# Layer 2's recurrence on two heads a tile: direction pairs become head pairs, and the inverse is folded into the step

## The chip, the cores and the metric

The kernel runs on one core of one Trainium2 chip. The metric is the device time of one execution in microseconds. The engines are TensorE (PE in the rows, PEld for its weight loads), VectorE (DVE), ScalarE (ACT), GpSimd (POOL) and SyncE (SP), which issues the transfers.

## The reference

Three transformer layers run on one sequence of 512 tokens, with 256 context tokens in the first two; the width is 1024. The change touches layer 2 only, a recurrence with 16 heads of 64, run forward and backward over the context and then over the sequence:

```python
def step(S, inp):                       # S: 64 x 64 for each head
    w_t, k_t, v_t, kk_t, kka_t = inp[:5]
    S = (S * w_t[:, :, None, :]
         - jnp.einsum('bhij,bhj->bhi', S, kk_t)[..., None] * kka_t[:, :, None, :]
         + v_t[..., None] * k_t[:, :, None, :])
    y = jnp.einsum('bhij,bhj->bhi', S, inp[5]) if emit else None
    return S, y
...
for d, reverse in enumerate((False, True)):
    s_ctx, y_c = wkv_scan(s0, decay_c, k_dc, v_c, kk_c, a_c, r_c, reverse)
    _, y_d = wkv_scan(s_ctx, decay, k_d, v, kk, a, r, reverse)
y = rwkv_readout(ys[0] + ys[1], r, dirs[0][1] + dirs[1][1], v, g, r_k, ln_g, ln_b, wo, h.dtype)
```

The readout normalizes y by head, adds a bonus (sum of r, k and r_k over a head, times v), multiplies by the gate g and projects by wo.

## The kernel before

The 768 steps are cut into 12 chunks of 64 (4 of the context, 8 of the sequence). Within a chunk the recurrence is a triangular solve, so that a chunk needs a few 64 x 64 products, the inverse of a unit triangular matrix, and one state that is passed on. A block is two heads; there are eight blocks. The scheduler of the framework orders each engine's instructions ahead of the run, from program order and a model of its own; tiles in pools with a number of buffers set which work may run ahead.

The features are made first (`features`): decays, keys, rates and r are projected, written to memory by head with the backward direction reversed (`rev`), and the values v are written by token (`vt`). While the value projections still run, `Scan.front(0)` starts. Then `layer1` calls `rest` for block 0, and `front(blk)`, `rest()` for the blocks 1 to 7.

`front` (L304 on) works on one head at a time with the two directions on the halves of the 128 partitions: it loads the head's tensors, scans the log decays (L361), takes their exponentials (P at L364, inverse decays at L366), makes keys and rates (L368 to L377), fills the tiles G with products (L387, L390), and makes the chunk products on TensorE (L329), which masks move from PSUM into G (L332, L337) and copies into Ld (L334, L335). Transposes (L344, L346) complete G. There are three sets of G (`self.hp[blk % 3]`), and two of Ld. The bonus sum goes through memory (`bd`).

`rest` (L408 on) masks Ld on GpSimd (L421), transposes it on VectorE so that 96 small triangles lie on the partitions (L422), inverts their 32 x 32 diagonal parts by 60 instructions on GpSimd (L427, L428), transposes back (L432, L433) and assembles the 64 x 64 inverses T from 32 x 32 matmuls in PSUM bank f (L443 to L457). `fold` multiplies T into the transposed keys and the outputs' products in place (L467, L471). Then come 12 steps: a chunk's values and state lie together in a tile ZU, filled by transfers (L483); a step is a first group of matmuls (L501) into a bank b of this block's parity, two copies (ScalarE L503, VectorE L504), a second group with an identity that carries the state (L508, L509), and two multiplies by the chunk's decay (L512). The output Y gathers in a bank y, of which there are two (L520). The last part copies Y (L524), makes the norm's statistics in the same bank (L530 to L541) and writes the block out (L546). For block 7 the output projection of the blocks 0 to 5 is woven between its steps (`interleave`, L1288), with its weights in the room that `scan.fp` has left.

The lines that set how far blocks may run ahead:

```python
self.p.psum_swap(("mm", "v"), b0=1, b1=1, y=2)
G = self.hp[blk % 3].tile([128, 8 if g else 4, 4, CH], F32, name="G", tag=f"G{g > 0}", bufs=4 if g else 2)
Ld = self.lp[blk % 2 == 0].tile([128, 32, 64], F32, name="Ld", tag="Ld")
ps = self.p.pt(f"b{blk % 2}")
```

## Time and profile before

| | us |
|---|---|
| median of three runs (3163.01 to 3174.26) | 3166.6 |
| the profiled execution | 3169.68 |
| its span, first to last instruction | 3167.8 |
| TensorE busy | 2825.9 |
| VectorE busy | 1786.6 |
| ScalarE busy | 1552.0 |
| GpSimd busy | 1138.5 |

The mean granted TensorE clock is 0.923 of full speed. The feature projections of layer 2 run from about 1050 to 1268 us of the span, front and values together to about 1400, the blocks of the recurrence to 1980. Times in the rows count from the span's start. A row of a timeline merges neighbouring instructions of one line ("x8"), and its duration goes to the end of the last; an fp32 matmul is two instructions. "Idle before" is the time in which an engine waited, with what ended it.

### The profile page before, as it was taken

Reading aid. Unit: us, or ns where it says so; the run is one execution under the profiler, and the core shown is the slowest. Engines: PE = TensorE matmul, PEld = TensorE weight load, DVE = VectorE, ACT = ScalarE, POOL = GpSimd, SP = SyncE. Lnnn points to the kernel's source line nnn. Section 1 sums busy time; section 2 is a strip of 40 time slices with the busy share of each in tenths; the row PEclk is TensorE's granted clock in tenths of the full one; section 3 lists DMA queues with packets and bytes.
Section 4 is the critical chain, followed back from the end, with each engine's and each line's share of the span. In section 5 each row is a group of like instructions: output and inputs, shape, how many; then the busy total and the mean of one; then the engine's idle time right before and its main releaser. Section 6 shows DMA issues by size and latency. Waiting matters only on the chain.

```text
span 3167.8 us, 50960 instructions
## 1 busy us (share of the span) xinstructions
PE 2825.9 (89%) x19290; PEld 2343.8 (74%) x19290; DVE 1786.6 (56%) x3557; ACT 1552.0 (49%) x3104; POOL 1138.5 (36%) x1500
## 2 busy tenths in 40 slices
PE   6999889999996899886777769699997999989999
PEld 6967778888885688764666658577876885678887
DVE  8466383444448725758688732644456654556364
ACT  3246556666664633554566532455543444544341
POOL 4013436667675212045666640245543110010000
PEclk9989989999998899987688879799998996999999
DMA  5323213333331565432223231244541220022222
GB/s 224 127 82 98 104 50 128 117 126 127 113 114 61 190 194 156 162 123 84 73 96 103 79 113 53 99 171 170 179 150 56 80 87 7 14 80 90 103 96 85
DMA packets 137589, 345.69 MB, mean 109 GB/s; under 512 B 16385, under 2 KB 48769, under 8 KB 120065
## 3 DMA queue, kind: packets, MB, share of 16 engines
q1 hardware_dynamic: 137344, 342.43, 31.6%
q8 instruction: 153, 2.51, 0.3%
q14 instruction: 92, 0.75, 0.1%
HBM read 293.35 MB, written 49.02 MB: 108 GB/s over the span
## 4 chain that ended last, share of the span: by engine, by line
PE 34%; DVE 8%; ACT 6%; POOL 5%; DMA 4%; issue 2%; SPq 0%; ACTq 0%; POOLq 0%; DVEq 0%
PE mm L590 7%; PE mm L591 7%; PE mm L592 7%; POOL acc L733 2%; DMA adaw<-in_ada_dram 2%; PE a L1288 2%; ACT wh L583 1%; PE st L1247 1%; PE a L329 1%; POOL M L428 1%; POOL Mt L427 1%; PE y L520 1%; DVE G L387 1%; PE a L1920 1%; PE a L1923 1%
## 5 line engine op out<-in xcount | busy, mean ns | idle before, releaser
L733 POOL TENSOR_TENSOR acc<-acc,adat 128x256 f32<-128x256 f32 x658 | 574.9, 896 | 539.2 <-ACT acc L729 434.0
L584 DVE TENSOR_TENSOR wl<-wr,wh 128x2048 fp32r<-128x2048 f32 (+3 forms) x145 | 317.6, 2190 | 361.1 <-ACT wh L583 358.7
L732 ACT ACTIVATE adat<-adaw,silu 128x256 f32<-128x256 f32 x644 | 319.4, 508 | 262.9 <-POOL acc L733 164.0
L583 ACT CAST wh<-wr 128x2048 fp32r<-128x2048 f32 (+2 forms) x147 | 266.8, 1815 | 232.1 <-PE mm L591 218.7
L590 PE MATMUL mm<-fh,wh 128*128 128x512 f32 (+1 forms) x1008 | 350.2, 356 | 14.0 <-DVE relu L1015 9.8
L591 PE MATMUL mm<-fl,wh 128*128 128x512 f32 (+1 forms) x1008 | 353.1, 352 | 2.2 <-DVE fl L597 2.2
L592 PE MATMUL mm<-fh,wl 128*128 128x512 f32 (+1 forms) x1008 | 352.0, 351 | 0.9 <-DVE wl L584 0.9
L590 PE MATMUL mm<-h_xhi,wh 128*128 128x512 f32 (+1 forms) x784 | 277.7, 359 | 3.6 <-ACT h_xhi L596 2.5
L591 PE MATMUL mm<-h_xlo,wh 128*128 128x512 f32 (+1 forms) x784 | 278.2, 357 | 1.8 <-DVE h_xlo L686 1.5
L592 PE MATMUL mm<-h_xhi,wl 128*128 128x512 f32 (+1 forms) x784 | 278.1, 357 | 0.0
L664 POOL TENSOR_TENSOR acc<-acc,t 128x256 f32<-128x256 f32 x127 | 109.1, 867 | 345.0 <-ACT t L662 342.2
L590 PEld LDWEIGHTS mm<-fh,wh 128*128 128x128 f32 x1008 | 192.1, 191 | 42.1 <-DVE relu L1015 12.1
L591 PEld LDWEIGHTS mm<-fl,wh 128*128 128x128 f32 x1008 | 191.7, 190 | 27.6 <-DVE fl L597 4.0
L592 PEld LDWEIGHTS mm<-fh,wl 128*128 128x128 f32 x1008 | 192.0, 191 | 26.2 <-DVE wl L584 1.1
L1039 DVE TENSOR_TENSOR y<-mm,y 128x512 f32<-128x512 f32 (+1 forms) x184 | 99.5, 559 | 152.1 <-PE mm L592 151.6
L590 PE MATMUL mm<-h_hi,wh 128*128 128x512 f32 (+1 forms) x408 | 160.7, 398 | 6.3 <-ACT h_hi L685 6.3
L592 PEld LDWEIGHTS mm<-h_xhi,wl 128*128 128x128 f32 x784 | 149.0, 190 | 21.4 <-issue 0.2
L590 PEld LDWEIGHTS mm<-h_xhi,wh 128*128 128x128 f32 x784 | 147.6, 190 | 23.3 <-ACT h_xhi L596 2.8
L591 PEld LDWEIGHTS mm<-h_xlo,wh 128*128 128x128 f32 x784 | 148.9, 191 | 20.8 <-DVE h_xlo L686 1.7
L427 POOL TENSOR_TENSOR Mt<-M 128x30 f32<-128x30 f32 (+14 forms) x240 | 141.7, 591 | 58.1 <-PE f L443 23.6
L591 PE MATMUL mm<-h_lo,wh 128*128 128x512 f32 (+1 forms) x408 | 160.3, 394 | 0.0
L592 PE MATMUL mm<-h_hi,wl 128*128 128x512 f32 (+1 forms) x408 | 159.6, 393 | 0.0
(451 smaller groups left out, 6929.6 us busy)
## 6 DMA issues: line engine op xcount, KB each, us to landing
adaw<-in_ada_dram SPq DMA_DIRECT2D x256, 256.0 KB, 2.7
wr<-in_w_dram SPq DMA_DIRECT2D x64, 1024.0 KB, 4.8
wr<-in_wup_dram SPq DMA_DIRECT2D x22, 1024.0 KB, 4.7
base<-b SPq DMA_DIRECT2D x32, 384.0 KB, 3.1
ZU<-vt SPq DMA_DIRECT2D x192, 64.0 KB, 2.5
wr<-in_wdn_dram SPq DMA_DIRECT2D x16, 704.0 KB, 4.1
wr<-in_win_dram SPq DMA_DIRECT2D x9, 1024.0 KB, 4.7
wr<-in_evin_dram SPq DMA_DIRECT2D x8, 1024.0 KB, 4.8
```

Source lines behind the costliest of these rows:

```text
L329: nc.tensor.matmul(ps[:, c], bk[g][:, c0 + c].rearrange("p a t -> p (a t)"), G[:, :na, c0 + c, :], start=True, stop=True)
L427: nc.gpsimd.tensor_tensor(t, a, b, ALU.mult)
L583: nc.scalar.copy(hi[:, :n], raw[:, :n])
L584: (eng or nc.vector).tensor_tensor(lo[:, :n], raw[:, :n], hi[:, :n], ALU.subtract)
L590: mm(out, lhs[0], rhs[0], start=first, stop=False)
L591: mm(out, lhs[0], rhs[1], start=False, stop=False)
L592: return mm(out, lhs[1], rhs[0], start=False, stop=last)
L664: nc.gpsimd.tensor_tensor(acc, acc, sq, ALU.add)
L732: nc.scalar.activation(t, w, AF.Copy, scale=s)
L733: nc.gpsimd.tensor_tensor(acc, acc, t, ALU.add)
L1039: nc.vector.tensor_tensor(yb, ps[:, :n], yb, ALU.add)
L1288: bi = nc.tensor.matmul(ps[:, :256], wcol(m, k), z[:, k, o], start=k == 0, stop=k == early - 1)
```

## The change

The two halves of the 128 partitions now hold the two heads of a block, in all tiles, and both directions are made from the same loaded tensors, read backwards where needed; so nothing is stored twice, `rev` goes, and the second LoRA weights are dense with each direction on 64 rows. `front` loops over the directions: keys and rates are made in place in one tile bk, the products go by head into two PSUM banks, one mask each moves them into tiles tw on 128 partitions, and the lower part of the transposed triangles goes from there into Ld, which needs no mask on GpSimd. The bonus sum stays in a PSUM bank until both directions are in, and then in a tile.

`rest` loads all values of a block at once (V), inverts as before, assembles T in bank f, and multiplies it into separate tiles FX. A step has no tile that joins values and state: the values' shares of U and of the next state are summed first (`begin`, `zbegin`), the state's share and an identity are added, one ScalarE copy takes U to X, FX times X is added to the next state's bank, and one VectorE multiply makes Z. The values' share of Y is summed ahead of the steps. There are two sets of P, Ld and the front's output tiles, two banks u, one z, one y; the norm's statistics go to bank f. Before the output projection of block 7, `hp[0]` is given back together with `fp`.

The diff, cut to its core (the inversion, its constants, the input preparation and the stores of the features are left out, and of `front` and `rest` mostly the new lines stand):

```diff
-        self.hp, self.lp = {0: self.pool("sc_h0", 1, "right")}, {True: self.pool("sc_l0", 1, "right")}
+        self.hp = {0: self.pool("sc_h0", 1, "right")}
...
+    def fixed(self, i):
+
+        nc = self.nc
+        P = self.P[i] = self.cp.tile([128, 2, NT // CH, 1 + CH], F32, name=f"P{i}")
+        nc.vector.memset(P[:, :, :, 0:1], 1.0)
+        Ld = self.Ld[i] = self.cp.tile([128, 32, 32], F32, name=f"Ld{i}")
+        nc.gpsimd.memset(Ld[:, 24:, :], 0.0)
@@ -277,11 +274,12 @@
     def late(self):
 
         nc = self.nc
-        self.p.psum_swap(("mm", "v"), b0=1, b1=1, y=2)
+        self.p.psum_swap(("mm", "v"), u=2, z=1, y=1)
         self.cp = self.pool("sc_c1", 1)
-        self.tmp, self.zp = self.pool("tmp", 3), self.pool("sc_z", 2)
-        self.lp[False] = self.pool("sc_l1", 1)
-        self.hp[1], self.hp[2] = self.pool("sc_h1", 1), self.pool("sc_h2", 1)
+        self.tmp, self.zp = self.pool("tmp", 3), self.pool("sc_z", 3)
+        self.vp, self.xp = self.pool("sc_v", 2), self.pool("sc_x", 1)
+        self.hp[1] = self.pool("sc_h1", 1)
+        self.fixed(1)
@@ -304,122 +302,108 @@
...
+        NP, NPC = NT // CH, NC_ // CH
+        fp, hp, P, Ld = self.fp, self.hp[blk % 2], self.P[blk % 2], self.Ld[blk % 2]
+        v3 = lambda t: t.rearrange("p (c t) -> p c t", t=CH)
+
+        def load(name, n, src, bufs=None):
+            t = fp.tile([128, n], F32, name=name, tag=name, bufs=bufs)
+            nc.sync.dma_start(t, src)
+            return t
+
+        k, kk, r = load("kin", NT, self.p.kd[blk]), load("kkin", NT, self.p.kkd[blk]), load("rin", NX, self.p.rd[blk])
+
+        order = (lambda t: ((slice(0, NT), t),),
+                 lambda t: ((slice(0, NC_), t[:, NC_ - 1::-1]), (slice(NC_, NT), t[:, :NC_ - 1:-1])))
+
+        brk = hp.tile([128, 128], F32, name="brk")
+        nc.gpsimd.tensor_scalar(brk, self.bdiag, self.p.col("rk", blk), None, ALU.mult)
+        bon = self.p.pt("a")
+        TW, A = [], []
+        for d in range(2):
+            s, ta = load("sg", NT, self.p.sd[blk, d]), load("ta", NT, self.p.td[blk, d])
             cs = fp.tile([128, NT], F32, name="cs", tag="cs")
             nc.vector.tensor_tensor_scan(cs, self.mreset, s, 0.0, ALU.mult, ALU.add)

+            nc.scalar.activation(P[:, d, :, 1:], v3(cs), AF.Exp, scale=-C0)
             nc.scalar.activation(cs, cs, AF.Exp, scale=C0)
+
+            bk = fp.tile([128, NP, 3, CH], F32, name="bk", tag="bk", bufs=2)
+            f = bk[:, :, 1, :]
+            nc.scalar.activation(f, v3(ta), AF.Identity, scale=self.al[:, blk:blk + 1], bias=self.be[:, blk:blk + 1])
+            for o, t in order[d](kk):
+                nc.vector.scalar_tensor_tensor(ta[:, o], ta[:, o], 1.0, t, ALU.add, ALU.mult)
+            for o, t in order[d](k):
+                c = slice(o.start // CH, o.stop // CH)
+                nc.vector.tensor_tensor(f[:, c], f[:, c], v3(t), ALU.mult)
+            pr = fp.tile([128, NX], F32, name="prod", tag="sg")
+            nc.vector.tensor_tensor(v3(pr), v3(r if d == 0 else r[:, ::-1]), f[:, NPC:], ALU.mult)
+            nc.tensor.matmul(bon, brk, pr if d == 0 else pr[:, ::-1], start=d == 0, stop=d == 1)
+            nc.vector.tensor_tensor(bk[:, :, 0, :], v3(ta), v3(cs), ALU.mult)
+            nc.vector.tensor_tensor(f, f, v3(cs), ALU.mult)
+            nc.scalar.copy(bk[dr[1], :, 2, :], bk[dr[1], :, 0, :])
+
+            ac, al = hp.tile([128, NPC, 1, CH], F32, name=f"ac{d}"), hp.tile([128, NP - NPC, 2, CH], F32, name=f"al{d}")
+            ks = (kk[:, :NC_], kk[:, NC_:]) if d == 0 else (kk[:, NC_ - 1::-1], kk[:, :NC_ - 1:-1])
+            for t, x, ps in ((ac, ks[0], slice(0, NPC)), (al, ks[1], slice(NPC, NP))):
+                nc.vector.scalar_tensor_tensor(t[:, :, 0, :], v3(x), -0.5, P[:, d, ps, :CH], ALU.mult, ALU.mult)
+            nc.vector.tensor_tensor(al[:, :, 1, :], v3(r if d == 0 else r[:, ::-1]), P[:, d, NPC:, 1:], ALU.mult)
+
+            tw = [hp.tile([128, 8 if i else 4, 2, 3 if i else 2, CH], F32, name=f"tw{d}{i}") for i in range(2)]
+            side = lambda h, c: bk[dr[h], c, h:h + 2, :].rearrange("p a t -> p (a t)")
             for g in range(3):
+                na, t = (2, tw[1][:, g * 4 - 4:g * 4]) if g else (1, tw[0])
+                pss = [self.p.pt("a")[:, :4 * na * CH].rearrange("p (c a t) -> p c a t", c=4, a=na) for h in range(2)]
+                for c in range(4):
+                    for h in range(2):
+                        rhs = al[dr[h], (g - 1) * 4 + c] if g else ac[dr[h], c]
+                        nc.tensor.matmul(pss[h][:, c], side(h, g * 4 + c), rhs.rearrange("p a t -> p (a t)"), start=True, stop=True)
+                for h in range(2):
+                    mask = self.mscan.rearrange("p (a t) -> p a t", a=2)[:, :na].unsqueeze(1).to_broadcast([128, 4, na, CH])
+                    nc.vector.tensor_tensor(t[:, :, h, :na, :], pss[h], mask, ALU.mult)
+                if g == 1:
+                    continue
+
+                n, c0 = (8, 4) if g else (4, 0)
+                pts = [self.p.pt("a") for h in range(2)]
+                for c in range(n):
+                    for h in range(2):
+                        nc.tensor.transpose(pts[h][:, c * 64:(c + 1) * 64], side(h, c0 + c), ident[dr[h], dr[h]])
+                for h in range(2):
+                    nc.scalar.copy(tw[g > 0][:, :, h, na, :], pts[h][:, :n * 64].rearrange("p (c k) -> p c k", k=64))
+
+                for q in range(4):
+                    rows = slice(q * 32, q * 32 + 32)
+                    nc.scalar.copy(Ld[rows, d * NP + c0:d * NP + c0 + n], tw[g > 0][rows, :, q // 2, 0, q % 2 * 32:q % 2 * 32 + 32])
+            TW.append(tw)
+            A.append((ac, al))
+        vb = hp.tile([128, NX], F32, name="vb")
+        nc.scalar.copy(vb, bon)
+        self.now = blk, TW, A, vb
...
     def rest(self, z=None):
 
         nc = self.nc
...
+        blk, TW, A, vb = self.now
+        P, Ld = self.P[blk % 2], self.Ld[blk % 2]
+        tw = lambda d, p: TW[d][1][:, p - NPC] if p >= NPC else TW[d][0][:, p]
+        V = self.vp.tile([128, 2, NP, 64], F32, name="V")
+        for d in range(2):
+            for h in range(2):
+                cols = slice(blk * 128 + h * 64, blk * 128 + h * 64 + 64)
+                nc.sync.dma_start(V[dr[1 - h], d], self.p.vt[d, :, cols].rearrange("(c t) k -> t c k", t=CH))
 
...
+        F = sp.tile([128, 24, 32], F32, name="F")
+        for d in range(2):
...
+        FX = [self.xp.tile([128, 4, 2, 2 if g else 1, CH], F32, name=f"FX{g}") for g in range(3)]
+        for g in range(3):
+            for c0 in range(0, 4, 4 // n):
+                pp = self.p.pt("f").rearrange("p (c d k) -> p c d k", c=4 // n, d=2)
+                for c in range(4 // n):
+                        for h in range(2):
+                            nc.tensor.matmul(pp[dr[h], c, d], T[dr[h], d * NP + g * 4 + c0 + c, :],
+                                             tw(d, g * 4 + c0 + c)[dr[h], h, 1:].rearrange("p a k -> p (a k)"), start=True, stop=True)
+                nc.scalar.copy(FX[g][:, c0:c0 + 4 // n].rearrange("p c d a k -> p c d (a k)"), pp)
+        each = [(h, d) for h in range(2) for d in range(2)]
+        yc = lambda p, d: slice((p - 4) * 64, (p - 3) * 64) if d == 0 else slice((NP - 1 - p) * 64, (NP - p) * 64)
+        val = lambda h, d, p: V[dr[1 - h], d, p]
+        for p in range(NPC, NP):
+            for h, d in each:
+                nc.tensor.matmul(Y[dr[h], yc(p, d)], val(h, d, p), tw(d, p)[dr[1 - h], h, 1, ::1 - 2 * d], start=p == NPC and d == 0, stop=False)
+
+        def begin(p):
+            U = self.p.pt("u")
+            for h, d in each:
+                bi = nc.tensor.matmul(U[dr[h], d * 64:d * 64 + 64], tw(d, p)[dr[1 - h], h, 0], val(h, d, p), start=d == 0, stop=p == 0 and d == 1)
+            return U, bi
+
+        def zbegin(p):
+            zq = self.p.pt("z")[:, :128].rearrange("p (d k) -> p d k", d=2)
+            for h, d in each:
+                nc.tensor.matmul(zq[dr[h], d], tw(d, p)[dr[1 - h], h, 2 if p >= NPC else 1], val(h, d, p), start=d == 0, stop=False)
+            return zq
+
         steps = self.steps = []
+        Z, zq, (U, bi) = None, zbegin(0), begin(0)
         for p in range(NP):
+            g, c = p // 4, p % 4
+            at = [A[d][1][:, p - NPC] if g else A[d][0][:, p] for d in range(2)]
+            if 0 < p < NP - 1:
+                zq = zbegin(p)
+            if Z is not None:
+                for h, d in each:
+                    bi = nc.tensor.matmul(U[dr[h], d * 64:d * 64 + 64], at[d][dr[h], 0], Z[dr[h], d], start=False, stop=d == 1)
+            steps.append(bi.ins)
+            X = self.zp.tile([128, 2, 64], F32, name="X")
+            nc.scalar.copy(X, U[:, :128].rearrange("p (d k) -> p d k", d=2))
+            Zn = None
             if p + 1 < NP:
+                if Z is not None:
+                    nc.tensor.matmul(zq, self.p.cst("ident"), Z, start=False, stop=False)
+                U, bn = begin(p + 1)
+                for h, d in each:
+                    bi = nc.tensor.matmul(zq[dr[h], d], FX[g][dr[h], c, d, 1 if g else 0], X[dr[h], d], start=False, stop=d == 1)
                 steps.append(bi.ins)
+                Zn = self.zp.tile([128, 2, 64], F32, name="Z")
+                nc.vector.tensor_tensor(Zn, zq, P[:, :, p, CH:].to_broadcast([128, 2, 64]), ALU.mult)
+            if g:
+
+                for h, d in each:
+                    tk = slice(None, None, 1 - 2 * d)
+                    nc.tensor.matmul(Y[dr[h], yc(p, d)], Z[dr[h], d], at[d][dr[h], 1, tk], start=False, stop=False)
+                    nc.tensor.matmul(Y[dr[h], yc(p, d)], X[dr[h], d], FX[g][dr[h], c, d, 0, tk], start=False, stop=p == NP - 1 and d == 1)
+            Z = Zn
...
+        Y = self.p.pt("f")
         for tt in range(4):
             nc.tensor.matmul(Y[:, tt * 2:tt * 2 + 2], sq[:, tt * 128:(tt + 1) * 128], self.p.cst("sel64"), start=True, stop=True)
...
         for blk in range(1, 7):
             scan.front(blk)
             scan.rest()
-            if blk == 5:
-                scan.drop(scan.hp[2])
         scan.front(7)
         scan.drop(scan.fp)
+        scan.drop(scan.hp[0])
 
         wop = tc.alloc_tile_pool(name="l1w", bufs=1, side="right")
...
+            for i in range(16):
+                b, d = i // 2, i % 2
+                s, rows = slice(b * 128, (b + 1) * 128), slice(d * 64, d * 64 + 64)
                 for o, n in ((0, 512), (512, 256)):
                     ps = self.pt("mm")
...
-            rev(t, NT, b, self.b1, self.b0)
-            rev(kk, NT, b, self.b0, self.b1)
+            nc.sync.dma_start(self.kd[b], t)
+            nc.sync.dma_start(self.kkd[b], kk)
```

## Rows read from the trace of the kernel before

**Rows 1.** Busy time of each engine in three stretches (us, instructions), mean granted clock, DMA share.
```profile
1050.00:1268.00 218.00, 207.13 (x1128) 174.38 (x1127) 108.97 (x202) 100.23 (x180) 43.07 (x57) 0.98 0.59 184
...
1435.00:1835.00 400.00, 311.69 (x4203) 242.48 (x4203) 312.62 (x669) 228.00 (x545) 249.37 (x392) 0.81 0.27 86
...
1904.00:1980.00 76.00, 75.97 (x857) 61.30 (x857) 21.10 (x74) 19.01 (x50) 1.27 (x1) 1.00 0.17 52
```

**Rows 2.** One line's instructions, all eight blocks: durations, first and last start.
```profile
L422 DVE STREAM_TRANSPOSE M<-Ld x8: 1916/1941/1981, 1342.8 to 1834.5; 128x1024 f32<-128x1024 f32 x8
...
L524 ACT COPY ysb<-y x8: 567/586/587, 1504.6 to 1979.3; 128x512 f32<-128x512 f32 x8
...
L541 DVE SCALAR_TENSOR_TENSOR ysb<-ysb,cols,y x8: 740/746/749, 1519.4 to 1988.2; 128x512 f32<-128x512 f32 x8
```

**Rows 3.** Timeline: start, duration, engine, line; ScalarE, then VectorE, around 1810 and 1834.
```profile
1810.44 0.59 ACT L524 COPY ysb<-y 128x512 f32<-128x512 f32 x1 [0.77 <-PE y L520]
...
1834.49 1.95 DVE L422 STREAM_TRANSPOSE M<-Ld 128x1024 f32<-128x1024 f32 x1
```

**Rows 4.** Groups of instructions by form, 1268 to 1990 (busy, mean ns; idle before, releasers).
```profile
L512 DVE TENSOR_TENSOR ZU<-b,PC 64x128 f32<-64x128 f32 x176 | 50.6, 287 | 46.4 <-PE b L509 43.1
...
L387 DVE TENSOR_TENSOR G<-base,P 128x256 f32<-128x256 f32 x96 | 48.3, 536 | 4.7 <-PE b L509 2.3 <-PE y L520 1.8
...
L332 DVE TENSOR_TENSOR G<-a,c_mscan 64x128 f32<-64x128 f32 x128 | 36.2, 287 | 16.7 <-PE a L329 9.5 <-ACT Ld L335 4.4
...
L390 DVE TENSOR_TENSOR G<-rdup,P 128x512 f32<-128x512 f32 x32 | 28.1, 877 | 0.0
...
L504 DVE COPY ZU<-b 64x128 f32<-64x128 f32 x96 | 27.6, 293 | 61.7 <-ACT ZU L503 60.3
...
L337 DVE TENSOR_TENSOR G<-a,c_mscan 128x256 f32<-128x256 f32 x64 | 26.7, 422 | 7.5 <-ACT Ld L335 6.1
...
L371 DVE TENSOR_TENSOR ta<-ta,base 128x768 f32<-128x768 f32 x16 | 15.4, 961 | 1.5 <-ACT ta L369 1.4
...
L421 POOL TENSOR_TENSOR Ld<-Ld,c_mdiag 128x768 f32<-128x768 f32 x8 | 14.9, 1862 | 153.8 <-ACT Ld L335 137.9 <-DMA ta<-td 15.9
...
L1531 DVE TENSOR_TENSOR vt<-mm,vmean 128x512 f32<-128x512 f32 x12 | 8.3, 688 | 7.5 <-PE v L1542 7.3
```

**Rows 5.** The instructions that write or read tile M, all blocks.
```profile
L427 POOL TENSOR_TENSOR Mt<-M x240: 237/573/2035, 1344.9 to 1871.0; 128x30 f32<-128x30 f32 x8, 128x84 f32<-128x84 f32 x8, 128x130 f32<-128x130 f32 x8, 128x168 f32<-128x168 f32 x8
...
L432 DVE STREAM_TRANSPOSE Ld<-M x8: 1901/1934/1970, 1383.9 to 1871.6; 128x1024 f32<-128x1024 f32 x8
```

**Rows 6.** Timeline, block 0's assembly: first of TensorE's matmuls, last of ScalarE's copies.
```profile
1387.63 1.49 PE L443 MATMUL f<-Dd,Ld 32*32 32x32 f32 x48 [2.10 <-DVE Dd L433]
...
1401.34 0.95 ACT L457 COPY T<-f 32x384 f32<-32x384 f32 x2
```

**Rows 7.** Timeline, four steps of the last block, output projection (L1288) between.
```profile
1959.38 0.44 PE L501 MATMUL b<-ZU,G 128*64 128x64 f32 x7
...
1970.75 0.44 PE L501 MATMUL b<-ZU,G 128*64 128x64 f32 x7
...
1971.12 1.99 PE L1288 MATMUL a<-z,wo 128*128 128x256 f32 x8
...
1971.25 0.26 ACT L503 COPY ZU<-b 64x128 f32<-64x128 f32 x1
...
1971.54 0.29 DVE L504 COPY ZU<-b 64x128 f32<-64x128 f32 x1 [2.35 <-ACT ZU L503]
...
1973.33 0.34 PE L508 MATMUL b<-ZU,cst 128*64 128x64 f32 x4
...
1974.05 0.61 DVE L512 TENSOR_TENSOR ZU<-b,PC 64x128 f32<-64x128 f32 x2 [2.22 <-PE b L509]
...
1976.22 0.44 PE L501 MATMUL b<-ZU,G 128*64 128x64 f32 x7
```

**Rows 8.** Timeline: one group of fold matmuls in the steady part.
```profile
1604.56 1.09 PE L467 MATMUL f<-G,T 64*64 64x128 f32 x16
```

More of the change, by code (lines that the diff above doesn't have):

```diff
@@ L444, in rest @@
                                      start=True, stop=True)
[L445 to L448 removed]
+            for h in range(2):
+                b = h * 64 + 32
+                nc.scalar.copy(F[b:b + 32, us], fps[b:b + 32, :NP * 32].rearrange("p (c k) -> p c k", k=32))
             tps = self.p.pt("f")
             for p in range(NP):
[L451 to L454 removed]
@@ L455, in rest @@
-            for d in range(2):
-                b = d * 64 + 32
-                nc.scalar.copy(T[b:b + 32, hd * NP:(hd + 1) * NP, 0:32], tps[b:b + 32, :NP * 32].rearrange("p (c k) -> p c k", k=32))
-        def fold(g):
+                for h in range(2):
+                    b = h * 64 + 32
+                    nc.tensor.matmul(tps[b:b + 32, p * 32:(p + 1) * 32], Tt[b:b + 32, d * NP + p, :], F[b:b + 32, d * NP + p, :], start=True, stop=True)
+            for h in range(2):
+                b = h * 64 + 32
+                nc.scalar.copy(T[b:b + 32, us, 0:32], tps[b:b + 32, :NP * 32].rearrange("p (c k) -> p c k", k=32))
```

245 lines of the change are left out of this document (40 added, 205 removed).

## The prediction

> **What bounds the kernel now.** The change touches the second layer's recurrence, so I began with busy time by stretch [rows 1]. In the feature projections (1050 to 1268) TensorE is busy 207 of 218 us: that stretch is a matmul stretch. In the steady part of the recurrence (1435 to 1835) nothing is full: TensorE 312, VectorE 313, GpSimd 249, ScalarE 228 of 400 us, at a mean granted clock of 0.81. A stage in which four engines work 57 to 78% each is bound by a loop of waits, with queueing on top, so the next thing to read is how often a block comes and how long it lives. The evacuation of a block's output starts at 1504.6 for the first and 1979.3 for the last of eight [rows 2]: 67.8 us a block. A block lives from the transpose that opens its triangular inverse (first 1342.8, last 1834.5) to that evacuation: 162 us for the first, 145 for the last. So more than two blocks are in flight. What admits a new one is the set of G tiles, of which there are three: block 4's output leaves at 1810.4 and block 7, which takes over its set, opens its inverse at 1834.5 [rows 3], 24 us later; and the multiplies that fill G wait for the recurrence's matmuls (L387 for L509 and L520) [rows 4]. Three periods are 203 us, which is 24 plus a life of some 179. The loop is three blocks long, and its life is stretched by VectorE (400 us are 5.9 blocks, so 313/5.9 = 53 us a block), where a hop of the recurrence stands behind front work.
>
> **The change, part by part.** VectorE, by groups [rows 4]. Recurrence: L512 and L504 (50.6 + 27.6) become 11 Z multiplies a block of 0.29: 25, a saving of 53 over eight blocks. The G tiles: L387, L332, L390, L337 (48.3 + 36.2 + 28.1 + 26.7 = 139) become, per direction, two masks like L337 (0.42), four like L1531 (0.69), one 256-column and two 512-column products (0.42 and 0.8 each): 5.6, times 16 = 90, a saving of 49. The decay and key products now use all 128 lanes or go in one call of 768 columns (0.96, L371), for three of 256 before: 15 to 35 saved. Together 117 to 137, or 15 to 17 of the 53 us a block. ScalarE loses half its fold copies and 64-lane exponentials, near 8 us a block by the code. GpSimd loses L421 (1.86 a block) and gains a 128-column multiply; its 60-instruction inverse stays: 39.0 us the first time (1344.9 to 1383.9), 35.1 the last (1834.5 plus 1.9 to 1871.6) [rows 5], 249/5.9 = 42 a block in the stage, all in. TensorE gains: the steps have 286 small matmuls a block where there were 200. On SP a block's 24 loads of the values become 4, the input loads go from 10 to 7, and the bonus makes no trip through memory. None of these totals is the bound, so none of these savings is the gain.
>
> What sets the time is the new depth. (1) The sets of tiles go from three to two: decays P, Ld and the front's outputs of block k are those of k+2. The front of k+2 may load and scan, but its exponentials wait until the last step of k has read P, and all of it stands behind that. (2) The recurrence's banks are no longer doubled: u, z and y are shared by all blocks, and the output statistics now use bank f, which has one buffer and which the inverse's assembly and folds need. So those of block k+1 start only when the normalization of block k has read f. Before, they ran beside the previous block's steps. (3) In the front, the bonus sum holds one of the three banks a from its first direction to its second, so products and transposes pass through the other two, a pair at a time, each pair waiting for its evacuation.
>
> So block follows block in a serial chain: normalization + assembly and first fold + 12 steps.
> Normalization: 9.6 us for the last block of before (1979.3 to 1988.2 + 0.75) [rows 2], with a weight split of another stage in it; ends 8.5 and 14, taken 11, since the next front starts at the same instant.
> Assembly: 14.7 for the first block (1387.63 to 1401.34 + 0.95) [rows 6] with front work beside; the same 96 small matmuls and 8 copies now; ends 11.5 and 15 with the first fold, taken 15.
> Step: before, at its barest [rows 7], it is L501 0.44, copy 0.26, copy 0.29, L508 with L509 some 0.75, two multiplies 0.61, with 0.05 to 0.15 between: 2.6. Now: U 0.45 (with the next z group up to 0.7), one copy 0.26, fold matmuls 0.45, one multiply 0.29 and four hops of 0.1: 1.9 to 2.1 at full clock; the fall to half clock stretches the matmul part to about 3. Below 2.4 I don't go, as eight output matmuls and an identity matmul stand in the same queue. The other end is what one 2 us piece in one queue makes of it: L501 at 1970.75 to the end of the multiplies at 1974.66 is 3.9 with one run of eight output-projection matmuls (1.99) in between; 4.0. I take 3.0, as the front runs beside part of the steps: 36 a block.
> Sum: 11 + 15 + 36 = 62 a block, for 67.8.
> The loop of two: front after the exponentials (6 of VectorE, then per direction five rounds of two banks: matmuls 0.5 to 1.7, masks 0.84 or 1.4, copies 0.7 to 1.2, hops of 0.15, in all some 13; 33, ends 28 and 40), transposes 2 and 4, inverse 40, assembly 15, steps 36: 130, or 65 a block. It is the longer, and I take 65.
>
> **The sum over the stage.** First inverse opens at 1335 (8 of the 13 us that VectorE saves in front 0; ends 0 and 13); 2 + 39 + 4 to 1380, assembly 15, the values' load 4, 12 steps of 4.0 with front 1 beside: block 0 ends at 1447 (was 1504.6). Front 1 still waits for the room that the value projections give back: inverse at 1414, to 1458, assembly to 1473, steps 38: 1511. Five more blocks: 1836. Last block: 11 + 15, then 12 steps with the output projection between. Before, these go at 5.6 a step (1959.38 to 1976.22 over three [rows 7]) because TensorE is full (76 of 76 us in 1904 to 1980 [rows 1]); with 43% more small matmuls 6.0: 72, ending at 1934, for 1979.3: 45 us less. One new wait lies here: the projection's tiles now take the room of a front set that block 6 still uses, so the weights load only after block 6's normalization, while block 7's assembly runs: covered by those 15 us; uncovered, some 5 to 10. The features lose their reversing copies on GpSimd and half of two weight splits; TensorE is full there, so 0 (ends 0 and 4 faster). The rest does not change. Profiled execution 3169.7, less 45: 3125; the median of the runs is 3 us below that execution: 3122.
>
> **Rivals.** *Queues empty out* (faster): with 16 us less VectorE work a block the hops come bare: steps 29, normalization 8.5, assembly 11.5 make 49; the loop of two, with 28 for the front and 37 for the inverse, makes 56 and decides. Then blocks 0 and 1 end at 1431 and 1500, block 6 at 1780, block 7 at 1869: 110 less, 3057. For it: the last block, with no front beside it, has the shortest life and the shortest inverse [rows 2, 5]. Against: static order and the clock.
> *Lost depth costs more than the work saved* (slower): hops stay as crowded as now, steps at 4.0, normalization 14: 48 + 14 + 15 = 77 a block. With steps of 44 block 1 ends at 1517, and the stage at 1517 + 385 + 14 + 15 + 74 = 2005, 26 later: 3193. It decides from a period of 74, where 1511 + 5 x 74 + 98 is 1979. For it: today's overlap of neighbouring blocks is what hides these hops, and it goes.
> *Between them* lies no change: period 73 to 75, 3157 to 3176.
> *TensorE becomes the bound at a low clock* (slower): it is busy 312/5.9 = 53 us a block now at 0.81 [rows 1], some 43 at full clock, its short pauses included; 86 more step matmuls of two instructions of 0.03 (eight of L501 in 0.44 with their tail [rows 7]) make 48. At a mean clock of 0.65 that is 74 a block, and there it decides; at 0.6 it is 80, the stage ends at 2022, and the time is 3210. For it: the new matmuls are 64x64 and leave TensorE to wait for the serial chain. Against: fewer of them stand far apart when the period shrinks.
> *Row halves take turns* (less gain): the U and z groups write one bank from both row halves. If those took turns, each group would be some 0.2 longer, 5 us a block on the steps, 20 over the stage, as two blocks share them in the loop of two: 3142. Against it: the fold before writes one bank of f from both halves, and 16 of its instructions of 128 columns take 1.09 us [rows 8], where eight of 256 columns take 1.99 [rows 7], so in turn they would take about 2. The Trainium skill (TensorEngine Tiling (Array Packing), section Restrictions and Gotchas) says that different row tiles cannot access the same PSUM bank at the same time; the row shows no such turns.
>
> **How the numbers follow.** Forecast 0.43 (3090 to 3150), queues empty 0.24, row halves 0.03: faster 0.70. No change 0.08. Lost depth 0.16, low clock 0.06: slower 0.22. About 0.3% is what a measurement of this kernel can tell from no change. The range reaches from the bare-hop case with its tail bare as well (3050) to the lost-depth case (3195), and leaves out the low clock and the tails of both, under 2 in 10.
>
> **What would show it.** Right: evacuations of the output some 65 us apart; after each, the normalization's last multiply, then at once the 32x32 assembly matmuls that waited for it; the exponentials of front k+2 just after block k's last Z; VectorE near 37 us a block; 286 step matmuls. Steps of 3 us, of 2.4 in the fast rival and 4 in the slow one. Wrong: assembly of k+1 running before block k's output leaves, or a period set by GpSimd's inverses back to back, or TensorE without gaps at a low clock.

## The result: slower by 4.9%, nearly all of it in the recurrence

The changed kernel takes 3323.7 us (median of 4 runs, 3318.25 to 3327.71); the kernel before, on the same chip, 3167.2. The ratio is 1.049, 95% interval 1.047 to 1.052. The forecast was 3122 in a range of 3050 to 3195. The profiled execution of the changed kernel took 3327.7 us, its span 3325.9. Its lines are those of the changed file: L508 is the evacuation of a block's output (before L524), L406 and L416 the transposes that open and close the inverse (L422, L432), L525 the normalization's first multiply (L541), L498 the Z multiply, L421 the copies of the inverse, L330 the exponential that gives P.

One line's instructions in the profile of the changed kernel, all eight blocks: durations in ns, first and last start; below L416, what its engine stood for before it, in us and times:
```profile
L508 ACT COPY ysb<-y x8: 585/585/587, 1453.9 to 2133.9; 128x512 f32<-128x512 f32 x8
...
L406 DVE STREAM_TRANSPOSE M<-Ld x8: 1935/1974/2067, 1323.1 to 1987.7; 128x1024 f32<-128x1024 f32 x8
...
L416 DVE STREAM_TRANSPOSE Ld<-M x8: 1908/1911/2079, 1360.1 to 2024.4; 128x1024 f32<-128x1024 f32 x8
its engine sat idle before it (us, times) until:
  POOL M L412: 130.2, 8
```
Against [rows 2]: the first output leaves 51 us earlier, at 1453.9 for 1504.6, but the last 155 later, at 2133.9 for 1979.3; that is all but 3 of the 158 us between the two profiled executions. From first to last, an evacuation comes every 97.1 us (680 over 7) where it was 67.8. The last line is new: VectorE stood 130 us in front of the closing transposes, in eight waits of 16 on average. In the kernel before that line has no wait at all between 1435 and 1835.

Busy time of each engine by stretch, changed kernel, in the order of [rows 1]: TensorE, weight loads, VectorE, ScalarE, GpSimd, then granted clock. The three below are parts of one period:
```profile
1435.00:1835.00 400.00, 268.45 (x4282) 233.50 (x4278) 144.28 (x248) 124.86 (x261) 159.54 (x309) 0.64 0.17 44
...
1763.00:1801.00 38.00, 32.96 (x417) 29.13 (x414) 23.26 (x42) 18.23 (x39) 1.84 (x2) 0.50 0.21 71
...
1801.00:1820.00 19.00, 16.74 (x376) 13.85 (x374) 2.46 (x8) 4.49 (x12) 15.98 (x32) 1.00 0.09 24
...
1820.00:1840.00 20.00, 0.00 (x0) 0.00 (x0) 3.79 (x3) 0.15 (x1) 14.02 (x30) 0.54 0.00 0
```
Every engine does less than in [rows 1], so nothing is full; and in the last row 20 us pass in which TensorE does nothing; for the first 16 of them GpSimd works alone. What happens there, on VectorE, with the TensorE and ScalarE rows that belong to it (start, duration, engine, line; in brackets idle before and its releaser):
```profile
1754.92 0.29 DVE L498 TENSOR_TENSOR Z<-z,P 128x128 f32<-128x128 f32 x1 [1.91 <-PE z L495]
...
1799.45 1.96 DVE L406 STREAM_TRANSPOSE M<-Ld 128x1024 f32<-128x1024 f32 x1 [1.11 <-ACT Ld L379]
...
1814.99 0.29 DVE L498 TENSOR_TENSOR Z<-z,P 128x128 f32<-128x128 f32 x1 [1.62 <-PE z L495]
1816.90 0.29 DVE L498 TENSOR_TENSOR Z<-z,P 128x128 f32<-128x128 f32 x1 [1.62 <-PE z L495]
...
1818.33 0.45 PE L495 MATMUL z<-X,FX 64*64 64x64 f32 x8
...
1836.17 1.91 DVE L416 STREAM_TRANSPOSE Ld<-M 128x1024 f32<-128x1024 f32 x1 [18.98 <-POOL M L412]
1837.93 1.88 DVE L417 STREAM_TRANSPOSE Dd<-M 128x1024 f32<-128x1024 f32 x1
1839.67 0.29 DVE L498 TENSOR_TENSOR Z<-z,P 128x128 f32<-128x128 f32 x1
...
1839.85 3.35 ACT L421 COPY T<-Dd 32x768 f32<-32x768 f32 x4 [21.64 <-DVE Dd L417]
...
1844.30 0.29 DVE L498 TENSOR_TENSOR Z<-z,P 128x128 f32<-128x128 f32 x1 [4.34 <-PE z L495]
...
1850.07 0.29 DVE L498 TENSOR_TENSOR Z<-z,P 128x128 f32<-128x128 f32 x1 [2.20 <-PE z L495]
```
Seven steps of block 4 go through; the first three Z multiplies, with folds still running, start 3.6 and 2.8 us apart, the last four 1.8 to 1.9. The matmuls of the eighth are done at 1818.8, but its Z multiply starts at 1839.67. It needs nothing from the inverse. It stands behind it: in VectorE's queue the two closing transposes of block 5's inverse come between the seventh and the eighth Z multiply of block 4, and they wait for GpSimd until 1836. ScalarE's four copies of that inverse stand ahead of the next X copy in the same way: its matmuls are done at 1840.7, and it starts at 1843.2, 2.5 us later. Six of the eight blocks show this split, after the sixth or seventh step. (The Trainium skill, "PSUM — Partial Sum Buffer", Engine vs sequencer instructions, calls the queues of ScalarE, VectorE and GpSimd strict FIFO; the 20.9 us for which a ready multiply stood agree.)

That ties neighbouring blocks into a ring. From the last Z of block 3 (1754.92) front 5 runs to the opening of its inverse at 1799.45: 44.5. The inverse takes 36.7, to 1836.17. Transposes 3.5, to 1839.67; the last four steps of block 4 take 10.4, to 1850.07; and that Z lets front 6 begin. Sum 95.1, and 1850.07 - 1754.92 is 95.15. The loop holds one front and one whole inverse for every block, where the forecast had them once for two. The chain that ended last between 1740 and 1950 says the same by line:
```profile
by line: POOL M L412 15.2%; POOL Mt L411 14.3%; PE a L362 9.4%; issue 9.1%; DMA ta<-td 7.0%; ACT T L421 3.8%; DVE Dd L417 2.7%; PE z L495 2.2%; DVE bk L344 2.2%; PE y L503 2.2%; PE f L438 2.1%; PE f L611 2.0%; PE f L429 1.9%; ACT Ld L379 1.
```

### The profile page after: what moved, and what is told of

Read it like the earlier page. It is cut to its first block, busy times and chain, and to the rows that moved or that the text cites. A ratio compares the mean times of both kernels' runs of the same rounds, so it can differ in the third digit from the quotient of the medians.

```text
span 3325.9 us, 53211 instructions
## 1 busy us (share of the span) xinstructions
PE 2894.5 (87%) x21242; PEld 2431.2 (73%) x21242; DVE 1627.1 (49%) x3063; ACT 1471.5 (44%) x2849; POOL 1054.1 (32%) x1437
## 4 chain that ended last, share of the span: by engine, by line
PE 30%; POOL 8%; ACT 5%; DMA 4%; DVE 4%; issue 2%; SPq 0%; POOLq 0%; ACTq 0%; DVEq 0%
PE mm L574 6%; PE mm L575 6%; PE mm L576 6%; DMA adaw<-in_ada_dram 3%; POOL acc L717 3%; POOL M L412 2%; POOL Mt L411 2%; PE a L362 2%; ACT wh L567 1%; PE a L1270 1%; PE st L1231 1%; ACT adat L716 1%; PE a L1890 1%; PE b L1225 1%; PE a L1893 1%
## 5 line engine op out<-in xcount | busy, mean ns | idle before, releaser
L567 ACT CAST wh<-wr 128x2048 fp32r<-128x2048 f32 (+2 forms) x147 | 264.8, 1801 | 239.8 <-PE mm L575 217.2
L575 PEld LDWEIGHTS mm<-fl,wh 128*128 128x128 f32 x1008 | 191.6, 190 | 29.1 <-DVE fl L581 5.7
L411 POOL TENSOR_TENSOR Mt<-M 128x30 f32<-128x30 f32 (+14 forms) x240 | 116.9, 487 | 240.2 <-DVE M L406 133.4
L473 PE MATMUL z<-V,tw 64*64 64x64 f32 x704 | 46.2, 254 | 130.3 <-DVE Z L498 128.0
```

The source lines that it names most:

```text
L411: nc.gpsimd.tensor_tensor(t, a, b, ALU.mult)
L567: nc.scalar.copy(hi[:, :n], raw[:, :n])
L575: mm(out, lhs[0], rhs[1], start=False, stop=False)
```

## Experiments

The theory: VectorE's queue (Q). The rivals: the lost third set (D), and the shared banks (S). "Period" below is the evacuations' first to last start, over seven; it was 67.8 before and 97.1 in the changed kernel. It contains the last block, which carries the output projection; from the second to the seventh evacuation alone a block takes 93.9 in the changed kernel and 64.5 before. Ratios are to the kernel before, run beside each experiment on the same chip, where it took 3172 to 3179 us (3167 beside the changed kernel); differences of medians between runs on different chips carry that much, up to some 10 us.

### The inverse halved, order kept

```
-        for s in range(1, 31):
+        for s in range(1, 31, 2):
```
Every second round of the inversion is left out. The transposes and copies are tied to the seventh Z and X.

> Leaves out every second pair of the inverse's multiply and add on GpSimd (16 instructions fewer in 15 of the 30 rounds, some 18.4 of its 36.7 us a block); that part of the computation is missing. The two back-transposes and the four copies of the inverse are held to the place where the changed kernel has them, behind the seventh Z multiply and X copy of the block before, so the order of the queues is the same. Theory Q (VectorE's queue makes the loop one block long: front of block k+2, its inverse, its back-transposes, the last four steps of block k+1 behind them): each us taken from the inverse comes off each period, 94.5 to 76, and the time is near 3195 (3175 to 3215). Rival D (only the lost third set: the loop is two blocks long and holds one inverse): half of it, 9 us a block, near 3260. Rival S (serial chain over the shared banks: normalization, assembly, steps): the inverse is not in it, 3315 to 3325.

Measured: 3230.6 us, 93 less than the changed kernel; between the second and the sixth evacuation 78.5 a block, for 94.3 in the changed kernel. The inverse with its opening went from 36.7 to 19.4, so 15.8 of the 17.3 us came off every period: the inverse is in the loop whole, as Q says, neither half (D) nor absent (S). The total missed its range (3175 to 3215): the first output left 15 us later than in the changed kernel, and the last block gained 1.

### The order alone: transposes behind the last Z

```
+        for late, last in zip((back, tops), self.last):
+            for i in late if last is not None else ():
+                self.p.tc.add_manual_dep(i.ins, last, order_only, reason="behind")
```
`order_only` is a dependency without a semaphore, `back` are L416 and L417, `tops` the copies; `last` are the last Z multiply and the squares of the block before.

> One edit to the changed kernel, in the order alone: the two back-transposes of a block's inverse stand on VectorE behind the last Z multiply of the block before, and its four copies on ScalarE behind that block's squares. Same sets, same banks, same instructions. Theory Q: the one-block loop of 95 opens. What is left is the loop of two blocks, 41 (front) + 37 + 4 (inverse and transposes) + 3 (copies) + 17 (assembly) + 28 (folds and steps) = 130, or 65 a block, to 72 where the normalization of a block, which still stands behind the next block's back-transposes, waits for them: 22 to 29 less a block over seven blocks, 3120 to 3170. Rivals D (lost set) and S (shared banks): neither is touched, 3300 to 3330.

Measured: 3250.2 us, ratio to before 1.023 (1.021 to 1.025); period 84.8. Faster than the changed kernel by 74 us with the order alone, but 80 above the upper end that Q had named. The timeline of VectorE shows why:
```profile
1700.26 0.29 DVE L502 TENSOR_TENSOR Z<-z,P 128x128 f32<-128x128 f32 x1 [1.62 <-PE z L499]
1712.07 1.90 DVE L416 STREAM_TRANSPOSE Ld<-M 128x1024 f32<-128x1024 f32 x1 [11.52 <-POOL M L412]
1713.83 1.86 DVE L417 STREAM_TRANSPOSE Dd<-M 128x1024 f32<-128x1024 f32 x1
1715.57 0.39 DVE L351 SCALAR_TENSOR_TENSOR ac<-kkin,P 128x256 f32<-128x256 f32 x1
```
The steps now run through, and the next front (L351, ready after the exponentials near 1701) stands behind the transposes instead. I had named what the transposes would no longer block, and not what they would block next.

### The same edit, one place further: behind the normalization

The edit above with `last` set to the multiply that reads bank f (L525 in the changed kernel).

> As the kernel with the back-transposes behind the last Z, but they now stand behind the first multiply of the block's normalization that reads bank f, so that the front of block k+2 and the normalization of block k no longer wait on VectorE for the inverse of block k+1; the four copies stand on ScalarE behind the squares. Theory Q in full (both places in VectorE's queue cost: 14 us a block behind the steps, the rest behind the front): what is left is the chain over the shared bank, 17 (normalization) + 4 + 3 (transposes, copies) + 15 (assembly) + 8 (folds to the first multiply) + 22 (steps) + 2 = 71 a block, 3140 to 3180. Rival D (two sets make a loop of 162 us over two blocks, wherever the transposes stand, as in the old kernel with two sets): 81 a block stays, 3235 to 3255.

Measured: 3193.3 us, ratio to before 1.005 (1.003 to 1.007); period 78.0, and VectorE's wait before the transposes falls to
```profile
  POOL M L412: 5.0, 2
```
That is 13 above the range expected. So 130 of the 157 us that the changed kernel lost to the one before (by the ratios 4.4 of 4.9%) came back by the place of two instructions in VectorE's queue, and of four in ScalarE's; how much is due to those four was not tried. Q holds in the main; D, that the time stays near 3245 wherever the transposes stand, does not.

### What depth costs by itself: the old kernel with two sets

```
-                G = self.hp[blk % 3].tile([128, 8 if g else 4, 4, CH], F32, name="G", tag=f"G{g > 0}", bufs=4 if g else 2)
+                G = self.hp[blk % 2].tile([128, 8 if g else 4, 4, CH], F32, name="G", tag=f"G{g > 0}", bufs=4 if g else 2)
```

> The kernel before with two sets of G tiles instead of three and nothing else changed: what the lost depth costs by itself. Old loop of two: 24 us from an output's evacuation to the next inverse on the same set, inverse and transposes 46, assembly 15, folds and steps some 50: 135, or 67 a block, which is what it has now. Theory Q: depth by itself costs little, 3165 to 3210. Rival D: the loop of three blocks lasts 203 us and keeps its length over two blocks, 80 to 100 a block, 3250 to 3390.

Measured: 3245.4 us, ratio 1.021 (1.018 to 1.024):
```profile
L524 ACT COPY ysb<-y x8: 563/586/590, 1494.2 to 2060.7; 128x512 f32<-128x512 f32 x8
```
A period of 80.9, 13 us above 67.8: above Q's expectation, and at the lower end of D's per block. Depth is not free. In the old kernel the third set was worth 71 us; its closing transposes wait 9.6 us in all there, so that is not the wait of Q. The new kernel, with the order put right, takes 3193 on two sets, 52 less than the old one on two; that its smaller work makes the difference is likely and not shown. A third set for the new kernel was not tried, so what the lost set costs there stays open.

### Statistics back in bank y

```
-        Y = self.p.pt("f")
         for tt in range(4):
```

> Undoes one part of the change: the output statistics and the broadcast of the normalization go back to bank y, so bank f is free for the next block's assembly. With this edit the planner also puts the back-transposes behind all eleven Z multiplies of the block before (seven in the changed kernel). Rival S (shared bank f sets the period): faster, by the 17 us of normalization a block, 3200 or less, and faster than the kernel in which only the order is changed. Theory Q: faster because the order changed, near the kernel in which only the order is changed, 3120 to 3180; in every other block the four copies of the inverse stand ahead of the output's evacuation on ScalarE, which costs some of it. Rival D (lost set): 3300 to 3330.

Measured: 3267.9 us, period 88.7, 18 slower than with the order alone and 75 slower than behind the normalization. The edit also moved the transposes, behind the last Z, where VectorE waits 136.1 us in all before them. None of the three ranges was met: the run says that a free bank f does not lift the loss, and no more on the bank.

### The depth eased: chunk-end decays copied out

```
+            nc.vector.tensor_copy(PC[:, d, :], P[:, d, :, CH])
-                nc.vector.tensor_tensor(Zn, zq, P[:, :, p, CH:].to_broadcast([128, 2, 64]), ALU.mult)
+                nc.vector.tensor_tensor(Zn, zq, PC[:, :, p:p + 1].to_broadcast([128, 2, 64]), ALU.mult)
```

> One edit to the changed kernel, against the depth: the 24 columns of P at the ends of the chunks, the only ones that the steps read, are copied out in the front (2 copies of 128x12 a block, as the kernel before had them), and the Z multiplies read the copy. So the exponentials and products of front k+2 no longer wait for the last step of block k; only what writes ac, al and tw does. The back-transposes stay ahead of the last five or six Z multiplies. Theory Q: the loop of one block stays, shorter by the part of the front that moves out of it, the two exponentials, the reload of ta (5.2 us) and the products, some 15 to 20 of 41: 75 to 80 a block, 3185 to 3225. Rival S (shared banks): nothing, 3315 to 3330.

> Both edits at once: chunk-end decays copied out, back-transposes behind the normalization. If the chain over the shared banks is what is left (71 a block), copying the decays out adds little to the order alone: 3130 to 3175. If the loop of two blocks still sets the time in the kernel with the order alone, this is 20 us a loop, 10 a block, faster than that one.

> Chunk-end decays copied out, and the output statistics back in bank y, so that the next block's assembly need not wait for the normalization. The planner then puts the back-transposes behind ten or all eleven Z multiplies of the block before. Theory Q: front 20 to 25 after the last step, inverse 37, transposes 4, with the front and the inverse in turn on VectorE's queue: 62 to 70 a block, 3090 to 3160. If the shared bank f is the rest of the cost, this one beats the kernel with the decays out and the back-transposes behind the normalization.

Measured: alone 3315.0, with the statistics in y 3294.9, and with the transposes behind the normalization 3175.8 us, ratio to before 1.000 (0.999 to 1.002). Alone it missed its expectation by 90 us: the front's exponentials did run ahead, but the transposes stayed in front of Z multiplies (VectorE waits 112.2 us before them) and the period was 91.0. The ring is still there: from block 3's last Z to the opening of inverse 5 it takes 32.3, 12 less, but the inverse takes 42.3, with the front's VectorE work now beside it, and after the transposes (3.6) six steps stand where there were four, 14.6; that makes 92.7. With the statistics in y as well the miss is 135 us above the range; the transposes stand before the last one or two Z multiplies there, and VectorE waits 116.5 us. Together with the order the edit takes 17 us more off and equals the kernel before, where I had expected 10 a block, 70 in all, of a loop of two blocks. The normalization, 18 to 20 us after the evacuation without this edit, then comes after 6.7, because the front's products no longer stand ahead of it. The closing transposes have stopped waiting: in blocks 2 to 7 the inverse ends 2 to 11 us before them, and they stand for their place behind the normalization.

### Three more places

> Chunk-end decays copied out, and the back-transposes behind the last Z multiply of the block before instead of behind its normalization. In the kernel with both edits the inverse of block 4 ended near 1683 and its back-transposes stood until 1699.9 behind the normalization, while block 3's last Z was at 1690.5. If the chain from normalization to assembly is what is left there, 5 to 8 us a block come off: 68 a block, 3115 to 3150, faster than the kernel before. If instead the loop of two blocks is what is left (the next front waits again behind the transposes), nothing or a loss: 3170 to 3200.

> The same with the output statistics back in bank y. By the rows of the last kernels the normalization takes 6.7 us and the transposes with their copies 9 to 14, so bank f would be free in time and this changes little: within 20 us of the kernel with the statistics in bank f, 3110 to 3165. If the shared bank f still holds the assembly up, it is 30 us or more faster than that one.

> As the kernel with the decays copied out and the back-transposes behind the normalization, but they stand behind the first VectorE instruction of the normalization (variance plus epsilon) instead of its last, 4 us earlier. If chain steps trade one for one, transposes 4 us earlier and normalization 4 us later cancel: 3165 to 3185. If the front's place in the queue decides, as it did behind the last Z multiply (3212), 3190 to 3220.

Measured, all with the decays out: transposes behind the last Z 3211.6; the same with the statistics in y 3254.4; behind the normalization's first instruction 3191.8 us. The first two expectations are missed by 60 us and more: I took the chain alone and left out again what would stand behind the transposes, the normalization and the front (VectorE waits 39.6 and 67.7 us before them). The third falls in the range for the case that the place in the queue decides: four microseconds of place, from the first instruction of the normalization to its last, are worth 16 us of the total.

### A second bank f

```
-        self.p.psum_swap(("mm", "v"), u=2, z=1, y=1)
+        self.p.psum_swap(("mm", "v"), u=1, g=1, z=1, y=1)
-            fps = self.p.pt("f")
+            fps = self.p.pt("fg"[d])
```

> The kernel with the chunk-end decays copied out and the back-transposes behind the normalization, with one more edit: bank u single instead of double, and the bank that this frees used as a second f (assembly of direction 1 and every other group of folds in it), so that matmuls and evacuations of the assembly and the folds overlap. If the chain over bank f is what is left (assembly 17, folds to the first multiply 9 to 11 of some 73 a block), 5 to 8 us a block come off, and a single bank u gives back up to 3: 3125 to 3165, faster than the kernel before. If two sets of tiles are the bound, 3170 to 3185.

Measured: 3198.5 us (12 runs, 3177 to 3202), ratio 1.006 (1.004 to 1.008), slower than the 1.000 without it and above both ranges. In the period shown, the assembly and folds shrank as meant (from the first 32x32 matmul to the first Z multiply 19 us, for 28 before), but the steps gave it back: from the first to the last Z 44 us for 32. Their stretch, without and with the second bank:
```profile
1658.00:1691.00 33.00, 27.66 (x512) 23.94 (x514) 7.88 (x18) 7.74 (x22) 27.74 (x49) 0.74 0.08 26
```
```profile
1660.00:1705.00 45.00, 34.80 (x549) 28.09 (x544) 16.90 (x29) 13.14 (x30) 32.76 (x52) 0.66 0.11 37
```
More of the front now falls among the steps (VectorE 16.9 us there for 7.9), at a lower clock. Which share is the single bank u's was not separated, so nothing is decided on bank f.

### A shorter front

Since the decays are copied out, the second P is needless; its room takes s and ta of direction 1, whose reload stood in the front.
```
+            q = self.tp if blk and d else fp
-            s, ta = load("sg", NT, self.p.sd[blk, d]), load("ta", NT, self.p.td[blk, d])
+            s, ta = load("sg", NT, self.p.sd[blk, d], q=q), load("ta", NT, self.p.td[blk, d], q=q)
```

> As the kernel with the decays copied out and the back-transposes behind the normalization (period 65 to 75 us), with the inputs s and ta of direction 1 in buffers of their own, in the room of the second P, which the copied decays make needless. Their reload, some 5 us that both directions of a front share one buffer for, stood in the chain that ended last (sg and ta: 5 to 8% of it). If the loop of two blocks holds the time, with the front in it, 2 to 5 us a block come off: 3135 to 3165, faster than the kernel before. If the serial chain (normalization, transposes, assembly, folds, steps) holds it, it stays at 3165 to 3185.

> The same with the back-transposes behind the last Z multiply. There the inverse ended after the last Z and VectorE stood for it; a front shorter by the reload opens the inverse some 5 us earlier. If the loop of two holds the time, 3170 to 3195 (it was 3212 without the own buffers), still behind the kernel with them behind the normalization, because the front stands behind the transposes again.

Measured: behind the normalization 3154.3 us, ratio to before 0.992 (0.990 to 0.995); behind the last Z 3202.2. The first:
```profile
L517 ACT COPY ysb<-y x8: 586/586/587, 1452.8 to 1957.5; 128x512 f32<-128x512 f32 x8
```
A period of 72.1, for 74.0 without the own buffers: this version is 0.8% faster than the kernel before, and its time is in the range that I had named for the loop of two. By the trace that hit is luck, for the loop of two is not what held the time. The inverse ends first, and VectorE stands at the transposes for nothing but the normalization ahead of them (GpSimd's last multiply, then VectorE):
```profile
1671.60 0.25 POOL L417 TENSOR_TENSOR M<-M,Mt 128x30 f32<-128x30 f32 x1
```
```profile
1673.59 0.75 DVE L534 SCALAR_TENSOR_TENSOR ysb<-ysb,cols,f 128x512 f32<-128x512 f32 x1
1674.25 1.92 DVE L421 STREAM_TRANSPOSE Ld<-M 128x1024 f32<-128x1024 f32 x1
```
In blocks 2 to 7 it ends 0.3 to 4.6 us before them. What got shorter is the serial chain, as the front's work stands among its folds and steps: from the transposes to the first Z multiply 31.0 us, for 33.4 without the own buffers, and from the first to the last Z 29.1, for 32.0 (block 4 here, block 3 there). Behind the last Z the total missed its range by 7 us.

## Why the prediction was wrong, step by step

**The step that failed** is "the loop of two: ... 130, or 65 a block". Its terms are a walk along data: P free, front, inverse, assembly, steps. Dividing by two supposes that the other block's work flows beside it. But VectorE does the front, the closing transposes and the Z multiplies in one queue, and where the transposes of block k+1 stand among the Z multiplies of block k, a link is added that no data asks for, and the loop is one block long. The prediction told of (1) depth, (2) banks and (3) the bonus, and named for no instruction of the inverse what would be queued behind it on VectorE and ScalarE. What the runs showed in its place is the ring of 95 above, with one whole inverse and one front for every block, and 130 us back when the place alone was changed. The rows of before couldn't show the wait: its closing transposes wait for nothing between 1435 and 1835, and with two sets for 9.6 us in all. But the place in the queue could have been asked for, and its price had rows: an inverse of 35 to 39 us [rows 5].

**Terms mis-sized.** With the order put right, evacuations come every 78.0 us where the forecast's own first and last (1447 and 1934 over seven) gave 69.6; that and a first block 10 later make 69 of the 202 us between forecast and result. Normalization: 11 taken, 18.2 measured in the changed kernel (evacuation at 1758.84, its multiply from 1776.24 for 0.75), as the next front's products stand ahead of it on VectorE: the matmuls of the statistics end at 1762.4, and VectorE first reads them at 1769.5. Front: 33 taken behind the exponentials (ends 28 and 40), 44.5 measured with them (1.7); in 1763 to 1801 the granted clock is 0.50, the lower level, and TensorE is busy 33 of 38 us, after 4 of 22 us in the stall before it (1720 to 1742) and 14 of 21 between the two. Some 5 us of it is the reload of ta, which I had put nowhere. Steps: 3.0 taken and a floor of 2.4 drawn, 1.92 measured where neither front nor folds cross, as the bare sum (1.9 to 2.1) had it; drawing the floor above it was wrong.

**Steps that held.** Assembly 15: 14.5 (1780.19 to 1794.71). Inverse 40 with its opening: 36.7. Exponentials of front k+2 right after block k's last Z: 0.3 us after it (1755.25 and 1754.92). VectorE near 37 us a block: 144.28 in 400 us at 94.3 a block is 34. The last block, 98 from the evacuation of block 6 forecast, takes 94 (2040.3 to 2133.9), with its middle steps at 5.3 to 6.0, for 6.0:
```profile
2085.95 0.29 DVE L498 TENSOR_TENSOR Z<-z,P 128x128 f32<-128x128 f32 x1 [5.03 <-PE z L495]
2091.29 0.29 DVE L498 TENSOR_TENSOR Z<-z,P 128x128 f32<-128x128 f32 x1 [5.05 <-PE z L495]
2097.30 0.29 DVE L498 TENSOR_TENSOR Z<-z,P 128x128 f32<-128x128 f32 x1 [5.72 <-PE z L495]
```

**The rivals.** "Queues empty out" named bare steps, and they came, at 1.92, but did not set the time. "Lost depth" had the sign, and depth has a price (71 us in the old kernel), but its mechanism, steps at 4.0, was not seen where no inverse stands in the way. "TensorE the bound at a low clock": the clock did fall, to 0.64, yet TensorE is busy 268 of 400 us, so it is not the bound; how much the low clock after the stall lengthened the front was not measured. (That rival's 2022 for a period of 80 doesn't follow from its own terms: 1511 + 5 x 80 + 98 is 2009.) "Row halves take turns": eight instructions from both row halves into one bank take 0.45 us (the row at 1818.33), for 0.44 of seven full-row ones in [rows 7], so no time is lost to turns. None of the rivals had the queue.

## What to carry to other kernels

When a change shortens the distance between the stages of a pipeline, write down for every instruction that waits long (here a transpose that waits for 35 us of GpSimd) what stands behind it in its engine's queue; a loop "of two blocks" is one only if no such instruction of one block stands in front of the other's work. Moving one out of the way moves it in front of something else, so name that too before counting the gain. Here the place of two transposes, with the four copies behind them, was worth 130 us.

## Not expected of the hardware

GpSimd's inverse, the same 60 instructions, got slower where VectorE had more work beside it. Busy times over one inverse each, in the changed kernel, with the transposes behind the normalization, and in the kernel before (VectorE's busy time is the third of those with a count behind them, GpSimd's the fifth, with one to six other instructions in it):
```profile
1801.00:1836.00 35.00, 16.74 (x376) 13.85 (x374) 2.46 (x8) 4.49 (x12) 29.86 (x61) 0.79 0.05 13
```
```profile
1657.00:1699.00 42.00, 33.43 (x667) 28.45 (x666) 20.96 (x36) 13.38 (x29) 36.75 (x62) 0.84 0.31 79
```
```profile
1702.00:1755.00 53.00, 44.13 (x594) 33.84 (x593) 43.99 (x95) 32.92 (x79) 42.10 (x66) 0.88 0.32 102
```
Of the inverse's own tile alone, 61 instructions in each, these are 29.9 us with VectorE all but still, 36.4 with 21 us of its work, 39.8 with 44. ScalarE's work and the transfers grow along in these rows, so they alone don't show whose doing it is. And the other way: a VectorE instruction on 8 columns, 0.17 us otherwise, took as long as the GpSimd multiply that had started 0.04 before it:
```profile
1771.79 1.26 POOL L523 TENSOR_TENSOR sq<-sq,vb 128x512 f32<-128x512 f32 x1 [30.52 <-DMA ta<-td]
```
```profile
1771.63 0.17 DVE L599 SCALAR_TENSOR_TENSOR rs_r<-rs_t,rs_r 128x8 f32<-128x8 f32 x1
1771.83 1.24 DVE L597 SCALAR_TENSOR_TENSOR rs_t<-rs_r 128x8 f32<-128x8 f32 x1
```
(The Trainium skill, "GPSIMD Engine Reference", Specifications, lists GpSimd's way to SBUF as shared with VectorE, with contention where a VectorE instruction has two inputs there; the last two views agree, and the same shows in two more blocks of that kernel, at 1.16 and 1.26 us.) An inverse that is overlapped better takes longer here: 40 to 41 us in the kernels with the transposes behind the normalization, where the changed kernel's stalls gave it 34.5.
